# The last norm of the final four token tiles: its reciprocal root moved from GpSimd to ScalarE and VectorE

## The chip, the cores and the metric

The kernel runs on one core of a Trainium2 chip. The metric is the device time of one execution in microseconds (us), as the median of three runs. TensorE (PE in the profile, PEld for its weight loads), VectorE (DVE), ScalarE (ACT) and GpSimd (POOL) work side by side and wait for each other by semaphores; SyncE (SP) issues the transfers, all of them on one queue (q1).

## The reference

The model is one decoder layer over 2048 tokens of width 1024, in float32: a gated linear attention, then a gated feed-forward block with a causal convolution. Each is followed by a residual and a layer norm:

```
def layer_norm(x, g, b):
    mu  = mean(x, -1);  var = mean((x - mu)**2, -1)
    return (x - mu) * rsqrt(var + 1e-5) * g + b

def post_norm_residual(x, cs, w_mod, b_mod, ln_gain, ln_bias, sublayer):
    shift, scale, gate = split(cs @ w_mod + b_mod, 3)
    y = sublayer(x * (1 + scale) + shift)
    return layer_norm(ALPHA * x + (1 + gate) * y, ln_gain, ln_bias)
```

What matters here is the very last step: the layer norm behind the down projection of the feed-forward block. Its result is the output.

## The kernel before

Every large product is made of three matmuls on a float32 operand that is split into a high and a low part (`split`, lines 107 to 111, and `mm3`, lines 113 to 116). The feed-forward block uses a seven-product scheme for 2 x 2 blocks (`ORDER`, `INTO`). The down projection (lines 1321 to 1381) walks over two halves `p` of the tokens and, in each, over the seven products `i`. A product fills four PSUM banks, one for each token tile `t` of 128 rows, and at its end `evict(t)` (line 1345) adds the bank to the accumulator `acc` in SBUF, one column half of 512 at a time.

For a product that completes a token tile (`whole`), the eviction also sums the row into `sm` (`accum_out`), and `ln2` (line 1299) makes the norm from that sum: GpSimd scales it, ScalarE squares and sums, GpSimd takes the power -1/2, VectorE makes the two column halves `y`, SP stores them. These `ln2` calls wait in a list, `work`, and are taken up between the matmuls of the next product.

The last product of the second half (`p == 1`, `i == 2`) is `outer`: here the loop over tiles is the outer one. The 33 matmuls of tile 0 come first, then its eviction and its norm, then tile 1, and so on; so only the norm of tile 3 has no matmuls behind it. Two of the four `ln2` calls that product 3 left in `work` are taken up inside tile 0, the other two inside tile 1. The norm of these last four tiles is `ln2_last` (line 1278). It takes mean and variance from `bn_stats` and `bn_aggr` on VectorE (the statistics of columns 0 to 511 are made ahead, line 1363), then calls `rsqrt_eps` (line 173), two GpSimd instructions: add 1e-5 (line 174), then the power -1/2 (line 175). Beside them VectorE makes (a - mean) * gain for both column halves (line 1290); then, for each half, times the reciprocal root plus the bias (line 1294) and a store (line 1295).

The eviction in `outer` carries the row sum too (line 1347), though `ln2_last` does not read it.

The program orders instructions by a planner: it simulates the engines, takes what is ready by the order of the text, and obeys the added edges of `order(later, earlier)` (line 76). Tiles come from pools. The pools on the left side of SBUF lie one behind the other, `const` first, then `smp`, `rawp`, `hlp`, `t2p`, `zp` and the pools of the stages (`ab`, later `up`); each small tile takes a multiple of 32 bytes per partition. The buffers of `rawp`, `hlp`, `t2p` and `zp` begin at multiples of 256 bytes. The tile `U` of the pool `up` has 1032 floats, 4128 bytes, and two buffers: the second begins 32 bytes past a multiple of 256. In the stage's first loads, the four pairs of `xs` (line 302 to 309) use these two buffers in turn. The pools `actp`, `ur` and `gp` lie on the right side.

Of the kernel before, what the change touches and what calls it, by code (L numbers as in the profile page):

```python
# [8 lines left out]
F32 = mybir.dt.float32  # L9
F32R = mybir.dt.float32r  # L10
U32 = mybir.dt.uint32
AF = mybir.ActivationFunctionType
ALU = mybir.AluOpType
# [3 lines left out]
P = 128  # L17
# [17 lines left out]
EPS = 1e-5  # L35
# [4 lines left out]
def kernel(  # L40
# [22 lines left out]
    nc = tc.nc  # L63
    load = nc.sync.dma_start
    store = nc.sync.dma_start

    const = ctx.enter_context(tc.tile_pool(name="const", bufs=1))
# [8 lines left out]
    def order(later, earlier):  # L76
        tc.add_manual_dep(later.ins, earlier.ins.name,
                          mybir.DependencyInfo(mybir.DependencyClass.NoSync, mybir.DependencyReason.DATA),
                          reason="issue order")
# [4 lines left out]
    def psum(tag, bufs=1):  # L84
        return ps.tile([P, 512], F32, tag=tag, name="ps_" + tag, bufs=bufs)
# [27 lines left out]
    def mm3(po, a, b, first, last, resumed=False):  # L113
        nc.tensor.matmul(po, a[0], b[0], start=first, stop=False, skip_group_check=resumed)  # L114
        nc.tensor.matmul(po, a[0], b[1], start=False, stop=False, skip_group_check=resumed)  # L115
        return nc.tensor.matmul(po, a[1], b[0], start=False, stop=last, skip_group_check=resumed)  # L116
# [52 lines left out]
    nc.vector.memset(still.bitcast(F32), 1.0)  # L169
    mhalf = const.tile([P, 4], F32, name="mhalf")  # L170
    nc.vector.memset(mhalf, -0.5)

    def rsqrt_eps(o, i):
        nc.gpsimd.tensor_scalar(o, i, EPS, None, op0=ALU.add)
        nc.gpsimd.tensor_tensor(o, o, mhalf[:, 0:o.shape[1]], op=ALU.pow)
# [202 lines left out]
    if True:  # L378
# [75 lines left out]
        for n, (dk, more) in enumerate(PE_ROWS):  # L454
            wk = mod_row(start[0][0], dk)
            for c in range(4):
                i = nc.tensor.matmul(pm0[:, c:c + 1], wk[:, c // 2, c % 2 * P:c % 2 * P + P], cs[:, dk:dk + 1],
                                     start=n == 0 and c == 0, stop=False, skip_group_check=True)
# [453 lines left out]
        for tb in range(NTB):  # L912
            last = tb + 1 == NTB
            b = 32 * tb
# [303 lines left out]
    outr = out.rearrange("(t p) d -> t p d", p=P)  # L1218
    ORDER = (0, 1, 4, 5, 6, 3, 2)

    def row(i):
        if i < 2:
            r = gp.tile([P, D], F32, tag="G", name="row0") if i == 0 else ur.tile([P, D], F32, tag="h3", name="row1")
            load(r, lnrow[i:i + 1].partition_broadcast(P))
            nc.vector.tensor_scalar(r, r, ALPHA, None, op0=ALU.mult)
            return r
        hs = []
        for half in range(2):
            hs.append(ur.tile([P, 512], F32, tag="hid", name=f"row{i}", bufs=6))
            load(hs[-1], lnrow[i:i + 1, half * 512:half * 512 + 512].partition_broadcast(P))  # L1230
        return hs
# [28 lines left out]
    def d_get(q):  # L1260
        while len(dloaded) < min(q + 4, len(groups)):
            d_load()
        while len(dready) < min(q + 3, len(groups)):
            d_split()
        return dready[q]
# [12 lines left out]
    def ln2_last(p, b, t):  # L1278
        a, sm = acc.pop((p, b, t))
        st = sts.pop()  # L1280
        nc.vector.bn_stats(st[:, 1], a[:, 512:1024])
        mv = smp.tile([P, 2], F32, tag="mv", name="mv")
        nc.vector.bn_aggr(mv, st)
        rs = smp.tile([P, 2], F32, tag="rs", name="rs")
        rsqrt_eps(rs[:, 0:1], mv[:, 1:2])
        ys = []
        for half in range(2):
            cs_ = slice(half * 512, half * 512 + 512)
            y = t2p.tile([P, 512], F32, tag="t2", name="y")
            nc.vector.scalar_tensor_tensor(y, a[:, cs_], mv[:, 0:1], rows[2][half], op0=ALU.subtract, op1=ALU.mult)  # L1290
            ys.append(y)
        for half in range(2):
            cs_ = slice(half * 512, half * 512 + 512)
            nc.vector.scalar_tensor_tensor(ys[half], ys[half], rs[:, 0:1], rows[3][half], op0=ALU.mult, op1=ALU.add)
            store(outr[p * 8 + b * 4 + t][:, cs_], ys[half])

    sts = []

# [26 lines left out]
    rows = [row(i) for i in range(4)]  # L1325
    work = [(init_acc, 0, b, t) for b in range(2) for t in range(4)]
    for p in range(2):
        bank = {"A": [None] * 4, "C": [None] * 4}
        for i in ORDER:
            kind, b, half, whole = INTO[i]  # L1330
            cs_ = slice(half * 512, half * 512 + 512)
            fresh = i in (0, 1, 4)
            ng = (NP + 1) // 2
            outer = p == 1 and i == ORDER[-1]

            def mms(t, gi, got):
                n = min(2, NP - 2 * gi)
                h, w = got
                for k in range(n):
                    o = k * 512  # L1340
                    mm3(bank[kind][t], (h[:, 0, o + t * P:o + t * P + P], h[:, 1, o + t * P:o + t * P + P]),
                        (w[:, 0, o:o + 512], w[:, 1, o:o + 512]),
                        fresh and gi == 0 and k == 0, gi == ng - 1 and k == n - 1, not fresh)

            def evict(t):
                a, sm = acc[p, b, t]
                acc_out = {"accum_out": sm[:, half:half + 1]} if whole else {}
                nc.vector.scalar_tensor_tensor(a[:, cs_], bank[kind][t], 1.0, a[:, cs_],
                                               op0=ALU.mult, op1=ALU.add, **acc_out)
                if outer:  # L1350
                    ln2_last(p, b, t)
                elif i in (3, 2):
                    work.append((ln2, p, b, t))

            if fresh:
                bank[kind] = [psum("mm" if kind == "A" else "w", 4) for t in range(4)]
            if i == 3 and p == 0:
                work += [(init_acc, 1, 0, t) for t in range(4)]
            if outer:
                got = [d_get(q + gi) for gi in range(ng)]  # L1360
                for t in range(4):
                    sts.append(smp.tile([P, 2, 6], F32, tag="bst", name="bst"))
                    nc.vector.bn_stats(sts[-1][:, 0], acc[p, b, t][0][:, 0:512])
                    for gi in range(ng):
                        mms(t, gi, got[gi])
                        if gi % 3 == 1 and work:
                            f, *a_ = work.pop(0)
                            f(*a_)
                    evict(t)
            else:  # L1370
                for gi in range(ng):
                    got = d_get(q + gi)
                    if work and (gi > 0 or work[0][0] is init_acc):
                        f, *a_ = work.pop(0)
                        f(*a_)
                    for t in range(4):
                        mms(t, gi, got)
                        if gi == ng - 1:
                            evict(t)
            q += ng  # L1380
        work += [(init_acc, 1, 1, t) for t in range(4)] if p == 0 else []
# [58 lines left out]
```

## Time and profile before

| | |
|---|---|
| median of 3 runs | 2142.64 us (2141.45 to 2144.62) |
| the profiled execution | 2140.49 us, of which the span from first to last instruction is 2138.5 us |
| granted TensorE clock | 0.999 |
| busy: PE, DVE, ACT, POOL | 99%, 66%, 42%, 5% of the span |

The profile is that of one execution. A start is counted from the first instruction. Where a timeline row has "x2", it holds two instructions, and its length is that of both. What stands in brackets is the idle time of the engine just before, and who ended it.

### The profile page before, as it was taken

The page shows a single profiled execution, that of the slowest core. Times are in us where ns is not written, and L with a number is a line of the kernel's source. Part 1 is how long each engine was busy: PE and PEld are TensorE (multiplying, and loading weights), DVE is VectorE, ACT ScalarE, POOL GpSimd, SP SyncE. Part 2 cuts the span into 40 slices and gives each one's busy share as a digit, 9 for nine tenths or more (in the row PEclk, how much of TensorE's full clock was granted, in tenths as well). Part 3 has the DMA queues.
Part 4 walks back from the last instruction along what each step waited for, and adds up shares of the span by engine and source line. Part 5 has one row for each costly group of instructions (what it writes and reads, how often), then busy time and mean ns, then how long its engine had stood idle before and what let it go on. Part 6 is the DMA issues. An engine that isn't in the chain of part 4 may idle for free.

```text
span 2138.5 us, 26756 instructions
## 1 busy us (share of the span) xinstructions
PE 2123.3 (99%) x9917; PEld 1770.1 (83%) x9917; DVE 1421.9 (66%) x2013; ACT 892.9 (42%) x1356; POOL 115.9 (5%) x258
## 2 busy tenths in 40 slices
PE   9999999999999999999999999999999999999998
PEld 7888888888888888888888888888888888888886
DVE  7876576434743553878777778666666797578557
ACT  4655453334333343544444454333333433344332
POOL 0010100010001000000000000000000000021003
PEclk9999999999999999999999999999999999999999
DMA  8577886665866766777855469878778897677662
GB/s 314 172 266 259 316 324 228 241 247 176 290 233 243 261 239 234 252 262 282 307 190 183 176 214 341 287 254 279 252 263 277 267 321 276 193 246 253 190 204 89
DMA packets 155106, 529.28 MB, mean 247 GB/s; under 512 B 17664, under 2 KB 21888, under 8 KB 134752
## 3 DMA queue, kind: packets, MB, share of 16 engines
q1 hardware_dynamic: 154976, 527.58, 70.2%
q8 instruction: 78, 1.28, 0.2%
q14 instruction: 52, 0.43, 0.1%
HBM read 364.72 MB, written 162.79 MB: 247 GB/s over the span
## 4 chain that ended last, share of the span: by engine, by line
PE 89%; DVE 4%; DMA 4%; ACT 2%; issue 1%; SPq 0%; POOL 0%; POOLq 0%; DVEq 0%; ACTq 0%
PE ps_mm L114 21%; PE ps_mm L116 21%; PE ps_mm L115 21%; PE ps_w L115 8%; PE ps_w L116 8%; PE ps_w L114 8%; DMA raw<-in_wab_dram 2%; DVE hl L111 1%; DMA mraw<-in_mws_dram 1%; PE ps_w L864 1%; ACT hl L108 1%; PE ps_w L813 1%; PE ps_w L622 0%; DVE macc L234 0%; DMA xraw<-in_xT_dram 0%
## 5 line engine op out<-in xcount | busy, mean ns | idle before, releaser
L114 PE MATMUL ps_mm<-xc,hl 128*128 128x512 f32 x704 | 274.3, 390 | 0.0
L115 PE MATMUL ps_mm<-xc,hl 128*128 128x512 f32 x704 | 273.9, 389 | 0.0
L116 PE MATMUL ps_mm<-xc,hl 128*128 128x512 f32 x704 | 273.9, 389 | 0.0
L114 PE MATMUL ps_mm<-xm,hl 128*128 128x512 f32 x496 | 195.0, 393 | 0.6 <-DVE v L111 0.6
L116 PE MATMUL ps_mm<-xm,hl 128*128 128x512 f32 x496 | 193.6, 390 | 0.0
L115 PE MATMUL ps_mm<-xm,hl 128*128 128x512 f32 x496 | 193.6, 390 | 0.0
L114 PEld LDWEIGHTS ps_mm<-xc,hl 128*128 128x128 f32 x704 | 132.1, 188 | 27.5 <-ACT u L1031 0.2
L116 PEld LDWEIGHTS ps_mm<-xc,hl 128*128 128x128 f32 x704 | 132.1, 188 | 27.4
L115 PEld LDWEIGHTS ps_mm<-xc,hl 128*128 128x128 f32 x704 | 132.1, 188 | 27.3
L1045 DVE SCALAR_TENSOR_TENSOR ct<-U,cw_sb,ct 128x512 f32<-128x512 f32 x176 | 131.7, 748 | 22.1 <-ACT ct L1039 20.6
L114 PE MATMUL ps_w<-xc,hl 128*128 128x512 f32 x352 | 136.9, 389 | 0.0
L115 PE MATMUL ps_w<-xc,hl 128*128 128x512 f32 x352 | 136.9, 389 | 0.0
L116 PE MATMUL ps_w<-xc,hl 128*128 128x512 f32 x352 | 136.9, 389 | 0.0
L108 ACT CAST dhl<-raw 128x1024 fp32r<-128x1024 f32 x57 | 60.0, 1052 | 153.2 <-PE ps_mm L116 96.0
L1031 ACT COPY u<-ps_mm 128x512 f32<-128x512 f32 x88 | 51.4, 584 | 154.9 <-PE ps_mm L116 153.0
L108 ACT CAST hl<-raw 128x1024 fp32r<-128x1024 f32 (+1 forms) x73 | 70.0, 966 | 106.0 <-PE ps_mm L116 42.3
L111 DVE TENSOR_TENSOR dhl<-raw,dhl 128x1024 fp32r<-128x1024 f32 x57 | 69.6, 1221 | 65.3 <-ACT dhl L108 65.3
L111 DVE TENSOR_TENSOR hl<-raw,hl 128x1024 fp32r<-128x1024 f32 (+1 forms) x73 | 81.0, 1118 | 47.9 <-ACT hl L108 47.8
L114 PEld LDWEIGHTS ps_mm<-xm,hl 128*128 128x128 f32 x496 | 93.3, 188 | 19.9 <-DVE v L111 1.0
L116 PEld LDWEIGHTS ps_mm<-xm,hl 128*128 128x128 f32 x496 | 93.2, 188 | 19.9 <-issue 0.2
L115 PEld LDWEIGHTS ps_mm<-xm,hl 128*128 128x128 f32 x496 | 93.3, 188 | 18.1 <-issue 0.2
L114 PE MATMUL ps_mm<-dhl 128*128 128x512 f32 x264 | 102.7, 389 | 0.0
(246 smaller groups left out, 4996.8 us busy)
## 6 DMA issues: line engine op xcount, KB each, us to landing
hl<-wq_d SPq DMA_DIRECT2D x82, 1024.0 KB, 5.0
hc_d<-ct SPq DMA_DIRECT2D x154, 256.0 KB, 2.6
raw<-hc_d SPq DMA_DIRECT2D x70, 512.0 KB, 4.4
draw<-wc_d SPq DMA_DIRECT2D x70, 512.0 KB, 4.8
wq_d<-hl SPq DMA_DIRECT2D x32, 1024.0 KB, 5.2
raw<-in_wab_dram SPq DMA_DIRECT2D x46, 512.0 KB, 5.8
wu<-in_wup_dram SPq DMA_DIRECT2D x44, 512.0 KB, 5.7
wg<-in_wup_dram SPq DMA_DIRECT2D x44, 512.0 KB, 4.1
```

The lines of the kernel that those rows point to most:

```text
L108: accs["copy"] = nc.scalar.copy(h, src)
L111: return nc.vector.tensor_tensor(l, src if lsrc is None else lsrc, h.bitcast(F32), op=ALU.subtract)
L114: nc.tensor.matmul(po, a[0], b[0], start=first, stop=False, skip_group_check=resumed)
L115: nc.tensor.matmul(po, a[0], b[1], start=False, stop=False, skip_group_check=resumed)
L116: return nc.tensor.matmul(po, a[1], b[0], start=False, stop=last, skip_group_check=resumed)
L813: nc.tensor.transpose(pt[:, s * P:s * P + P], on[:, s, e * P:e * P + P], ident)
L864: nc.tensor.transpose(pt[:, t * P:t * P + P], src, ident)
L1031: return t, nc.scalar.copy(t, po)
L1045: nc.vector.scalar_tensor_tensor(ct, U[:, o + i:o + i + 512], cw_sb[:, j, i:i + 1], ct, op0=ALU.mult, op1=ALU.add)
```

## The change

A constant tile `eps` of one column is added behind `mhalf`. In `ln2_last`, ScalarE takes the square root of variance + eps (the constant as its bias operand), VectorE the reciprocal of that; an `order` edge puts the reciprocal behind the first product of column half 0. Each column half is then finished and stored before the next is begun. In `evict`, the row sum is left out where `outer` holds. `rsqrt_eps` stays, for the norms of the attention and of the first residual.

```
     nc.vector.memset(mhalf, -0.5)
+    eps = const.tile([P, 1], F32, name="eps")
+    nc.vector.memset(eps, EPS)
...
         nc.vector.bn_aggr(mv, st)
+
         rs = smp.tile([P, 2], F32, tag="rs", name="rs")
-        rsqrt_eps(rs[:, 0:1], mv[:, 1:2])
+        nc.scalar.activation(rs[:, 1:2], mv[:, 1:2], AF.Sqrt, bias=eps)
         ys = []
         for half in range(2):
             cs_ = slice(half * 512, half * 512 + 512)
             y = t2p.tile([P, 512], F32, tag="t2", name="y")
-            nc.vector.scalar_tensor_tensor(y, a[:, cs_], mv[:, 0:1], rows[2][half], op0=ALU.subtract, op1=ALU.mult)
-            ys.append(y)
-        for half in range(2):
-            cs_ = slice(half * 512, half * 512 + 512)
-            nc.vector.scalar_tensor_tensor(ys[half], ys[half], rs[:, 0:1], rows[3][half], op0=ALU.mult, op1=ALU.add)
-            store(outr[p * 8 + b * 4 + t][:, cs_], ys[half])
+            i = nc.vector.scalar_tensor_tensor(y, a[:, cs_], mv[:, 0:1], rows[2][half], op0=ALU.subtract, op1=ALU.mult)
+            if half == 0:
+                order(nc.vector.reciprocal(rs[:, 0:1], rs[:, 1:2]), i)
+            i = nc.vector.scalar_tensor_tensor(y, y, rs[:, 0:1], rows[3][half], op0=ALU.mult, op1=ALU.add)
+            store(outr[p * 8 + b * 4 + t][:, cs_], y)
...
-                acc_out = {"accum_out": sm[:, half:half + 1]} if whole else {}
+                acc_out = {"accum_out": sm[:, half:half + 1]} if whole and not outer else {}
```

## Rows read from the trace of the kernel before

**Rows 1.** The page: span and busy time of each engine.
```profile
span 2138.5 us, 26756 instructions
PE 2123.3 (99%) x9917; PEld 1770.1 (83%) x9917; DVE 1421.9 (66%) x2013; ACT 892.9 (42%) x1356; POOL 115.9 (5%) x258
```

**Rows 2.** PE's waits: us in total, times, longest; first and last of nine.
```profile
PE ps_mm L657 <- ACT hl L108: 1.7, 1, 1.7
...
PE ps_mm L114 <- DVE z L843: 0.2, 1, 0.2
```

**Rows 3.** The timeline from the last matmuls on: start, us, engine, line, operation.
```profile
2130.26 0.39 PE L116 MATMUL ps_w<-hl 128*128 128x512 f32 x1
2130.68 0.69 DVE L1348 SCALAR_TENSOR_TENSOR acc<-ps_w,acc 128x512 f32<-128x512 f32 x1
2131.30 0.08 DVE L1348 DVE_READ_ACCUMULATOR acc<-ps_w,acc 128x1 f32 x1
2131.41 0.69 DVE L1281 BATCH_NORM_STATS2 bst<-acc 128x6 f32<-128x512 f32 x1
2132.14 0.21 DVE L1283 BATCH_NORM_AGGREGATE mv<-bst 128x2 f32<-128x12 f32 x1
2132.39 1.41 DVE L1290 SCALAR_TENSOR_TENSOR y<-acc,mv,row 128x512 f32<-128x512 f32 x2
2132.44 0.77 POOL L174 TENSOR_SCALAR rs<-mv 128x1 f32<-128x1 f32 x1 [3.30 <-DVE mv L1283]
2133.29 0.93 POOL L175 TENSOR_TENSOR rs<-rs,mhalf 128x1 f32<-128x1 f32 x1
2134.25 1.42 DVE L1294 SCALAR_TENSOR_TENSOR y<-y,rs,row 128x512 f32<-128x512 f32 x2 [0.45 <-POOL rs L175]
2135.03 0.99 SPq L1295 DMA_DIRECT2D out_dram<-y  x2
```

**Rows 4.** VectorE's timeline in tile 2: its last two instructions.
```profile
2129.18 1.41 DVE L1294 SCALAR_TENSOR_TENSOR y<-y,rs,row 128x512 f32<-128x512 f32 x2 [0.45 <-POOL rs L175]
```

**Rows 5.** Source line 1290: duration in ns, least/median/most.
```profile
L1290 DVE SCALAR_TENSOR_TENSOR y<-acc,mv,row x8: 745/749/753, 2112.2 to 2133.1; 128x512 f32<-128x512 f32 x8
```

**Rows 6.** Groups by line and shape: busy us, mean ns, idle us before.
```profile
L495 DVE TENSOR_TENSOR B<-lnc,md 128x8 f32<-128x8 f32 x1 | 0.2, 159 | 0.0
L171 DVE MEMSET mhalf<- 128x4 f32 x1 | 0.1, 62 | 0.0
L163 ACT ACTIVATE cs<-c_sb 128x8 f32<-128x8 f32 x1 | 0.2, 208 | 0.5 <-DMA c_sb<-in_cT_dram 0.5
L1039 ACT ACTIVATE ct<-U,cb_sb,cw_sb 128x512 f32<-128x512 f32 x88 | 71.6, 813 | 49.0 <-DVE U L326 48.4
L1049 ACT ACTIVATE ct<-ct 128x512 f32<-128x512 f32 x88 | 55.7, 633 | 68.8 <-DVE ct L1045 68.8
L724 ACT ACTIVATE sr<-ps_mm 128x512 f32<-128x512 f32 x32 | 19.1, 596 | 36.5 <-PE ps_mm L116 36.4
L724 ACT ACT_TABLE_LOAD x8 | 10.3, 1283 | 0.1
```

**Rows 7.** ScalarE's last instruction (2107 to 2140), and VectorE's aggregate of tile 0.
```profile
2108.56 0.18 ACT L1304 ACTIVATION_READ_ACCUMULATOR sq<-acc,lsm 128x1 f32 x1
2111.97 0.21 DVE L1283 BATCH_NORM_AGGREGATE mv<-bst 128x2 f32<-128x12 f32 x1
```

**Rows 8.** A window: busy us by engine, clock, DMA share, GB/s.
```profile
200.00:300.00 100.00, 98.46 (x469) 81.16 (x467) 70.77 (x110) 47.26 (x66) 6.40 (x18) 1.00 0.86 319
```

**Rows 9.** The chain, 0 to 60: its two transfers (start, us).
```profile
2.16 4.70 DMA mraw<-in_mws_dram
6.88 10.30 DMA mraw<-in_mws_dram
```

**Rows 10.** Loads into `U` buffers: first (847.7 to 848.2), second (864 to 866.6).
```profile
xs<-xm_d SPq DMA_DIRECT2D x1, 512.0 KB, 3.2
xs<-xt_d SPq DMA_DIRECT2D x1, 512.0 KB, 3.6
```

## The prediction

> **What bounds the kernel now.** I read the page first: PE is busy for 2123.3 of 2138.5 us [rows 1]. The view of PE's waits says the same from the other side: it waited nine times, from 1.7 us down to 0.2 [rows 2]. So VectorE, ScalarE and GpSimd count only where PE has nothing left to do, and that is behind the last matmul. The timeline there is one chain [rows 3]. The last matmul ends at 2130.65 (2130.26 + 0.39), the eviction of tile 3 starts at 2130.68, and until the span ends at 2138.5 there are 7.9 us in which nothing runs beside the chain. The chain is: eviction, statistics, aggregate, GpSimd's two instructions (0.77 and 0.93 us), two finishing products on VectorE (1.42 us for both), the last store. VectorE makes its first two products (2132.39, 1.41 for both) beside GpSimd, then waits 0.45 us. The norms of tiles 0 to 2 lie beside the matmuls of the next tile; that of tile 2 ends at 2130.59 (2129.18 + 1.41) [rows 4], 0.09 us before the eviction of tile 3 starts. That cover is thin, so what a norm costs VectorE in the earlier tiles must be watched too.
>
> **The change part by part.**
>
> The sum left out of the eviction. The eviction takes 0.69 us; its accumulator read starts at 2131.30 and takes 0.08, and the statistics start at 2131.41 [rows 3]. The statistics read what the eviction writes, so they must wait for its end in any case. A dependent pair on VectorE is seen just below: statistics end at 2132.10, aggregate starts at 2132.14, 0.04 us later. The eviction ends at 2131.37; plus 0.04 is 2131.41, the start that it has already. The read is hidden in that gap. I take 0; the other end is 0.11 us gained (all the time from the read's start to the statistics).
>
> The root on ScalarE. GpSimd started 0.09 us after the aggregate's end (2132.35 to 2132.44) [rows 3]; I take the same for ScalarE. No Sqrt of one column stands in the trace. The nearest row is the 128x8 ACTIVATE of 0.208 us; a column operand costs about 0.09 (0.813 with two of them against 0.633 with none) [rows 6]. That makes 0.30, and with 0.03 to hand over, the root is there at 2132.77. VectorE comes to the reciprocal only behind the first product, by the order edge: two products take 1.41 and one takes 0.749 [rows 3, 5], so the next instruction starts 0.66 after the first, at 2133.05. The root has 0.28 us to spare, so its cost is 0 on the path. If the cover goes, each microsecond beyond that is paid in full. Queued behind the waiting Sqrt on ScalarE is nothing but the next Sqrt: its last other instruction ends at 2108.74 [rows 7].
>
> The function table. ScalarE loads a table when it changes between groups of functions, 1.283 us each, and it does so ahead of the wait: at line 724 the load has 0.1 us of idle time before it, while the ACTIVATEs of that line waited 36.4 us for PE [rows 6]. Sqrt is used nowhere before, so one load is due. ScalarE is idle from 2108.74 to 2112.18, when tile 0's aggregate ends [rows 7]: 3.4 us, in which the load fits. Later tiles find the table there. On the path: 0. Other end: a load inside the last tile, 2132.44 + 1.28 + 0.30 + 0.03 = 2134.05 for the root, 1.00 us behind 2133.05.
>
> On this point the Trainium skill speaks against the change: "ScalarE: Activation LUTs", section "What ACT_TABLE_LOAD costs", has a switch to another set of functions cost a load and a drain, 2.66 us together, and counts sqrt in a set of its own. The trace agrees on the load (1283 ns) and does not show the drain. By the page's figure the switch would still fit into the 3.4 us; put into the last tile it would make the root 2.4 us late, and the estimate of the end 2.2 us later than before.
>
> The order of the column halves. Reciprocal at 2133.05. It is not in the trace; between the MEMSET of 0.062 and the aggregate of 0.21 the nearest is a small TENSOR_TENSOR of 0.159 [rows 3, 6]. I take 0.16. The product that finishes half 0 needs it: 2133.05 + 0.16 + 0.04 = 2133.25. The first product of half 1 depends on nothing: 0.66 later, 2133.91 to 2134.66. Its finish waits for it: 2134.70 to 2135.45. Before, it ended at 2134.25 + 1.42 = 2135.67 [rows 3]. Gain: 0.22 us. With the reciprocal at 0.06 it is 0.32, at 0.21 it is 0.17. The planner may also put the first product of half 1 ahead of the reciprocal, if it counts the root as late: then 2133.05 to 2133.80, reciprocal 2133.71 to 2133.87, finishes from 2133.91 and 2134.57, end 2135.32, gain 0.35.
>
> The stores. Both are issued by SP, 0.99 us for the two with the wait between them [rows 3]. The last is issued when the last finish ends, before and after; the first goes out 1.0 us earlier (half 0 done at 2134.00 instead of 2135.00), which moves nothing at the end. No DMA is added.
>
> Tiles 0 to 2. Each norm loses VectorE's wait of 0.45 and gains a reciprocal and one dependent gap, the same 0.22 net. That widens the 0.09 us margin and stays off the path. GpSimd loses eight instructions that nobody else waits for.
>
> The constant. One MEMSET of some 0.06 us on VectorE at the start, where it is idle later on, 0. Its column takes 32 bytes ahead of every pool on the left side, so raw, hl, z and most other buffers begin 32 bytes past a multiple of 256, as every second `U` buffer does already. The two `U` buffers bound what that costs a transfer: 3.2 us into the first, 3.6 into the second [rows 10], so between nothing and 12%, with other traffic in both. A transfer that is 12% longer would still be hidden while the 16 DMA engines are busy for 0.86 of a dense stretch [rows 8]: it takes 1 / 0.86, 16%, before they are full. Not hidden is the start, where the chain holds 15.0 us of transfers (4.70 + 10.30) [rows 9]: 12% is 1.8 us. I take 0, by the side of the 88% that would be hidden anyway and because the loads that the chain names (into `actp`) don't move.
>
> On the same point, the Trainium skill, "DMA: Bandwidth & Descriptors", section "How a descriptor splits into AXI transactions", lets a piece that doesn't begin at a multiple of 256 bytes cost one transaction more. For a row of 4096 bytes that is 17 for 16, 6%, so an estimate of 0.9 us at the start; the rows above neither show nor exclude it.
>
> **The sum.** 0 + 0 + 0 - 0.22 + 0 + 0. The profiled execution took 2140.49 us, 2.0 more than its span; after the change it would take 2140.27. The median of the runs shown is 2.15 above the profiled execution, and I carry that over: 2142.64 - 0.22 = 2142.4.
>
> **The rivals.**
> - Half 1 goes ahead of the reciprocal: gain 0.35, 2142.3. For it: the planner's choice is not visible beforehand. Against: the text's order and the root's 0.28 us in hand. Chance 0.17.
> - The tail keeps its length: the root takes 0.22 us longer than its cover (0.28 + 0.22 = 0.50 more than I took), because handing over to ScalarE and back costs more than it did with GpSimd. 2142.6. Against it: 0.09 us from VectorE to GpSimd [rows 3]. Chance 0.12.
> - The table is loaded in the last tile's chain: +1.00 - 0.22 = +0.78, 2143.4, slower. Against it: the load at line 724 runs before the wait, and three Sqrts come first. Chance 0.06.
> - The 32 bytes lengthen the transfers, slower than before: at the bound of 12% the start grows by 1.8 us, 2144.2. From 29% on (4.3 / 15.0) it would pass 0.2%, and from 16% on it would show as waits of PE between 200 and 300 us too. Chance 0.06, of which 0.03 above 0.2%.
> - The new instructions shift the planner's order far from the end, and PE's waits change by 5 us either way. PE's nine waits hold little that could be won [rows 2]: 0.01 faster; slower 0.01.
>
> My forecast has the remaining 0.57.
>
> **How the numbers follow.** What a measurement of this kernel can tell from no change is 0.2%, 4.3 us. All cases but the last and half of the one before lie within 2 us of the time before, that is, within 0.2%: 0.57 + 0.17 + 0.12 + 0.06 + 0.03 = 0.95. The runs of before spread over 3.2 us, and the profiled one lies 1 us below them, so a median of three can be off by itself; I move 0.02 of it outwards: faster 0.03, same 0.93, slower 0.04. The range takes the forecast, the rivals up to 2144.2 and the spread of the runs: 2140.0 to 2144.6.
>
> **What would show it.** In the changed profile: the statistics of tile 3 start 0.73 us after the eviction, with no accumulator read; a Sqrt of about 0.3 us beside the first product; one table load, before 2112; reciprocal 0.66 after the first product; the last finish 3.06 us after the first product starts, instead of 3.28. It would be wrong if the reciprocal idles for ScalarE, if VectorE is not done with tile 2 when the last matmul ends, or if PE's waits in the first 300 us grow.

## The result, and the profile after

| | median | runs | profiled execution / span |
|---|---|---|---|
| before | 2142.86 us | 2141.45 to 2144.62, 4 | 2140.49 / 2138.5 us |
| after | 2166.08 us | 2165.09 to 2167.15, 4 | 2167.15 / 2165.4 us |

The ratio after/before is 1.0111, 95% interval 1.0099 to 1.0123: the kernel became 23 us slower. The prediction of 2142.4 us was wrong, the measured time lies far above its range (up to 2144.6), and the case that had a chance of 0.93, no change, did not come. The two spans differ by 26.9 us. Two executions that took two and over five times as long as the rest, one of e4 (4239 us) and one of the kernel before on the chip of e5 to e8 (11932 us), are left out of every number below.

The page of the kernel after, span and busy time of each engine, answers to [rows 1]:

```profile
span 2165.4 us, 26752 instructions
PE 2153.0 (99%) x9917; PEld 1771.5 (82%) x9917; DVE 1423.9 (66%) x2014; ACT 895.7 (41%) x1361; POOL 109.6 (5%) x250
```

TensorE has as many matmuls as before, 9917, and is busy 29.7 us longer with them. The other engines' sums hardly moved. TensorE's waits after (total, times, longest; seven of them, first and last) leave nothing to explain it, as against [rows 2]:

```profile
PE ps_mm L434 <- DVE mhalf L171: 1.4, 1, 1.4
...
PE ps_mm L114 <- DVE v L111: 0.2, 1, 0.2
```

So the time went neither to waiting nor to more work. Where it went, the windows show (us, PE busy with its number of matmuls, PEld, DVE, ACT, POOL, granted clock, DMA share, GB/s). First the kernel before:

```profile
400.00:880.00 480.00, 479.54 (x2385) 403.45 (x2384) 231.40 (x382) 177.21 (x341) 29.39 (x68) 1.00 0.68 244
900.00:1700.00 800.00, 800.00 (x3548) 662.76 (x3547) 589.75 (x783) 331.29 (x448) 18.64 (x70) 1.00 0.73 255
1720.00:2080.00 360.00, 360.00 (x1590) 298.10 (x1589) 249.71 (x291) 149.32 (x166) 20.27 (x32) 1.00 0.72 240
```

and after, with the dense stretch of [rows 8] ahead:

```profile
200.00:300.00 100.00, 99.22 (x450) 79.75 (x449) 70.66 (x110) 46.24 (x65) 6.41 (x18) 1.00 0.86 319
400.00:880.00 480.00, 479.13 (x2357) 395.40 (x2357) 223.41 (x372) 172.98 (x338) 29.30 (x66) 1.00 0.66 237
900.00:1700.00 800.00, 800.00 (x3497) 653.55 (x3496) 585.22 (x780) 323.59 (x438) 21.88 (x75) 1.00 0.72 251
1720.00:2080.00 360.00, 360.00 (x1588) 297.82 (x1587) 258.16 (x302) 150.99 (x170) 20.93 (x32) 1.00 0.74 248
```

Read the count of matmuls in brackets. From 900 to 1700 us (the up projection) TensorE is busy in every microsecond of both kernels, at a granted clock of 1.00 in both, and got through 3548 matmuls before and 3497 after: 51 fewer, 1.4%. From 1720 to 2080 us, in the down projection, it is 1590 and 1588: no difference. A stretch from one run of 72 matmuls shows it too. TensorE's timeline after (start, length):

```profile
464.74 0.40 PE L114 MATMUL ps_mm<-hl,xm 128*128 128x512 f32 x1
464.98 0.39 PE L115 MATMUL ps_mm<-hl,xm 128*128 128x512 f32 x1
465.21 0.40 PE L116 MATMUL ps_mm<-hl,xm 128*128 128x512 f32 x1
465.44 0.39 PE L114 MATMUL ps_mm<-hl,xm 128*128 128x512 f32 x1
...
```

and the same in the kernel before:

```profile
458.16 0.39 PE L115 MATMUL ps_mm<-hl,xm 128*128 128x512 f32 x1
458.38 0.39 PE L116 MATMUL ps_mm<-hl,xm 128*128 128x512 f32 x1
458.61 0.39 PE L114 MATMUL ps_mm<-hl,xm 128*128 128x512 f32 x1
458.84 0.39 PE L115 MATMUL ps_mm<-hl,xm 128*128 128x512 f32 x1
...
```

A matmul's own length (0.39 to 0.40 us) says little, since they overlap; the distance from one start to the next is its price. I call this distance a step. Three of them take 0.70 us after (464.74 to 465.44) and 0.68 before (458.16 to 458.84); the mean over the 72 is 233.3 ns after and 226.8 before.

The end itself went almost as predicted. The timeline after from the last matmul on, against [rows 3]:

```profile
2156.61 1.41 DVE L1296 SCALAR_TENSOR_TENSOR y<-y,rs,row 128x512 f32<-128x512 f32 x2
...
2157.61 0.39 PE L116 MATMUL ps_w<-hl 128*128 128x512 f32 x1
2158.03 0.69 DVE L1350 SCALAR_TENSOR_TENSOR acc<-ps_w,acc 128x512 f32<-128x512 f32 x1
2158.76 0.69 DVE L1283 BATCH_NORM_STATS2 bst<-acc 128x6 f32<-128x512 f32 x1
2159.49 0.21 DVE L1285 BATCH_NORM_AGGREGATE mv<-bst 128x2 f32<-128x12 f32 x1
2159.73 0.29 ACT L1288 ACTIVATE rs<-mv,eps 128x1 f32<-128x1 f32 x1 [4.22 <-DVE mv L1285]
2159.73 0.75 DVE L1293 SCALAR_TENSOR_TENSOR y<-acc,mv,row 128x512 f32<-128x512 f32 x1
2160.40 0.16 DVE L1295 RECIPROCAL rs<-rs 128x1 f32<-128x1 f32 x1
2160.47 0.73 DVE L1293 SCALAR_TENSOR_TENSOR y<-acc,mv,row 128x512 f32<-128x512 f32 x1
2161.12 1.41 DVE L1296 SCALAR_TENSOR_TENSOR y<-y,rs,row 128x512 f32<-128x512 f32 x2
```

From the start of the eviction to the end of the last product it took 4.99 us before (2130.68 to 2135.67) and takes 4.50 now (2158.03 to 2162.53): 0.49 us won, in a kernel that lost 27 elsewhere.

### The profile page after: what moved, and what is told of

It is laid out like the page before. It is cut to its first block, busy times and chain, and to the rows that moved or that the text cites. A ratio compares the mean times of both kernels' runs of the same rounds, so it can differ in the third digit from the quotient of the medians.

```text
span 2165.4 us, 26752 instructions
## 1 busy us (share of the span) xinstructions
PE 2153.0 (99%) x9917; PEld 1771.5 (82%) x9917; DVE 1423.9 (66%) x2014; ACT 895.7 (41%) x1361; POOL 109.6 (5%) x250
## 4 chain that ended last, share of the span: by engine, by line
PE 91%; DVE 3%; DMA 3%; ACT 1%; issue 1%; POOL 0%; SPq 0%; DVEq 0%; ACTq 0%
PE ps_mm L114 22%; PE ps_mm L116 22%; PE ps_mm L115 22%; PE ps_w L115 7%; PE ps_w L116 7%; PE ps_w L114 7%; DMA raw<-in_wab_dram 1%; DMA mraw<-in_mws_dram 1%; PE ps_w L866 1%; PE ps_w L815 1%; DVE hl L111 0%; PE ps_w L624 0%; ACT hl L108 0%; DMA xp<-xm_d 0%; PE ps_w L545 0%
## 5 line engine op out<-in xcount | busy, mean ns | idle before, releaser
L114 PE MATMUL ps_mm<-xm,hl 128*128 128x512 f32 x496 | 197.5, 398 | 0.2 <-DVE v L111 0.2
L116 PE MATMUL ps_mm<-xm,hl 128*128 128x512 f32 x496 | 196.5, 396 | 0.0
L115 PE MATMUL ps_mm<-xm,hl 128*128 128x512 f32 x496 | 196.1, 395 | 0.0
L116 PEld LDWEIGHTS ps_mm<-xc,hl 128*128 128x128 f32 x704 | 132.2, 188 | 29.7
L115 PE MATMUL ps_w<-xc,hl 128*128 128x512 f32 x352 | 138.6, 394 | 0.0
L114 PE MATMUL ps_w<-xc,hl 128*128 128x512 f32 x352 | 138.6, 394 | 0.0
L116 PE MATMUL ps_w<-xc,hl 128*128 128x512 f32 x352 | 138.4, 393 | 0.0
```

## The experiments

Three theories stood at first; the expectations below go by their numbers. In the first two, the `eps` column is to blame, since it moves the buffers of the left side by 32 bytes. Theory 1, relative place: TensorE is slower wherever the moving operand (the one that streams through) lies on one side and the weights on the other, so that they no longer begin alike. Theory 2, absolute place: whatever begins 32 bytes past a multiple of 256 is slower by itself. Theory 3, the rival: the changed norms and evictions shift the planner's order far from the end. "+23" and the like below is the median less that of the kernel before on the same chip.

**e1: the column alone.** The kernel before, with the constant allocated and filled, and used by nothing.

```
     nc.vector.memset(mhalf, -0.5)
+    eps = const.tile([P, 1], F32, name="eps")
+    nc.vector.memset(eps, EPS)
```

> The kernel before with the eps column allocated and filled, and nothing else of the change: its value is not used. It moves the left-side buffers by 32 bytes. Theory 1, relative place: TensorE reads the moving operand of one matmul and the weights of the next at the same time, and a step costs 227 ns when both begin at the same remainder of bytes and 231 to 235 when one is 32 bytes off; so matmuls with one operand on the left and one on the right are slow: the whole loss stays, 2166 to 2167 us. Theory 2, absolute place: whatever begins 32 bytes past a multiple of 256 is slower to read or to transfer: 2166 to 2167 too. Theory 3, the new tail or the planner's order makes the loss: 2142.9.

Measured: 2165.24 us (2164.16 to 2166.61), ratio 1.0111 [1.0095, 1.0128]. Its window from 900 to 1700:

```profile
900.00:1700.00 800.00, 800.00 (x3497) 653.55 (x3496) 583.56 (x778) 322.87 (x438) 21.85 (x75) 1.00 0.72 251
```

The same 3497 matmuls as after. A column that nobody reads costs all of it.

**e2: the change without the column.** The whole change, with `eps` as a fifth column of `mhalf`, whose slot of 32 bytes has room for it; no buffer moves.

```
-    mhalf = const.tile([P, 4], F32, name="mhalf")
-    nc.vector.memset(mhalf, -0.5)
-    eps = const.tile([P, 1], F32, name="eps")
+    mhalf = const.tile([P, 5], F32, name="mhalf")
+    nc.vector.memset(mhalf[:, 0:4], -0.5)
+    eps = mhalf[:, 4:5]
...
```

> The whole change, but eps takes a fifth column of mhalf, whose 32 bytes it already has: no buffer moves. Theories 1 and 2: the loss is gone, 2142.4, and the tail from the last eviction to the last finish is 4.50 us instead of 4.99. Theory 3: 2166.

Measured: 2140.72 us (10 runs), ratio 0.9996 [0.9987, 1.0006], against 2141.61. The window from 900 to 1700:

```profile
900.00:1700.00 800.00, 800.00 (x3548) 662.76 (x3547) 589.30 (x782) 331.72 (x448) 18.74 (x70) 1.00 0.73 255
```

and VectorE's timeline in the norm of tile 3 (start, length, the idle time ahead in brackets):

```profile
2130.46 0.69 DVE L1350 SCALAR_TENSOR_TENSOR acc<-ps_w,acc 128x512 f32<-128x512 f32 x1 [0.60 <-PE ps_w L116]
2131.19 0.69 DVE L1283 BATCH_NORM_STATS2 bst<-acc 128x6 f32<-128x512 f32 x1
...
2133.55 1.41 DVE L1296 SCALAR_TENSOR_TENSOR y<-y,rs,row 128x512 f32<-128x512 f32 x2
```

All 3548 matmuls are back with the new norm in place, so the norm and the planner's order have no part in the loss. The built programs say the same: the matmuls of before, after, e1 and e2 stand in one and the same order, by the names and sizes of their operands. The tail takes 4.50 us as after (2130.46 to 2134.96). This is the version to keep: what the change was predicted to do, and no measurable difference in time, since 0.49 us is 0.02%.

**e3, e8: which side moves.** The right side ends in a pad of 56 floats. With 48, the buffers on the right (`actp`, `ur`, `gp`) begin 32 bytes higher. In e3 this is added to the whole change, so both sides moved by 32; in e8 it is the only edit to the kernel before.

```
-    pad.tile([P, 56], F32, name="pad")
+    pad.tile([P, 48], F32, name="pad")
```

> The whole change, and the pad tile on the right side 32 bytes smaller, so that the right-side buffers too begin 32 bytes past a multiple of 256. Theory 1: both operands have the same remainder again, steps of 227 ns, 2142.4 us. Theory 2: still more buffers are off, so 2166 or more, 2180 if the right side costs as much as the left. Theory 3: 2166.

> The kernel before with the right-side buffers moved up by 32 bytes and the left side where it was, 32 bytes the other way round than in the changed kernel. Theory 1: the same matmuls are slow: 2155 to 2166 us. If only the left side's place counts: 2142.

Measured: e3 2143.16 us (10 runs), 1.0007 [0.9998, 1.0017]; e8 2167.66 us, 1.0118 [1.0102, 1.0134]. The window of e3:

```profile
900.00:1700.00 800.00, 800.00 (x3547) 663.00 (x3546) 589.09 (x783) 331.06 (x447) 21.11 (x74) 1.00 0.73 255
```

and of e8:

```profile
900.00:1700.00 800.00, 800.00 (x3492) 652.27 (x3491) 583.24 (x777) 322.87 (x437) 21.88 (x75) 1.00 0.72 251
```

Either side alone costs 24 to 26 us, both together nothing that can be told. So it is not where a buffer begins that counts, but how the two sides lie to each other. It also excludes transfers as the cause: in e3 the buffers of both sides are moved by 32 bytes for their transfers too, and the time is back.

**e4, e5, e9, e10: by how much.** The whole change with one more constant, so that the left side moves by 64, 128, 96 and 160 bytes: 8, 24, 16 and 32 floats. e4's edit:

```
+    more = const.tile([P, 8], F32, name="more")
+    nc.vector.memset(more, 0.0)
```

> The whole change and one more unused constant of 32 bytes, so that the left-side buffers move by 64 bytes against the kernel before. Theory 1 with a period of 64 bytes: 2142.4 us; with a longer period (128 or 256): 2166, steps of 231 to 235 ns. Theory 2, with multiples of 256: 2166; theory 3: 2166.

> The whole change and one more unused constant of 96 bytes: the left-side buffers move by 128 bytes against the kernel before. Theory 1a, relative place with a period of 128 bytes: 2142 us. Theory 1b, a period of 256: slow, 2155 to 2166 us, with steps of 231 to 235 ns wherever one operand is on the left and one on the right. That 64 bytes cost less (2159) than 32 (2165) leaves both open.

> The whole change and one more unused constant of 64 bytes: the left-side buffers stand 96 bytes (of 256) off the right-side ones. Relative place with a period of 256: slow, 2155 to 2168 us, fewer matmuls than the 3548 of the kernel before from 900 to 1700 us. If only multiples of 32 that are not multiples of 64 cost the full price, it is near the 2165 of 32 bytes and not near the 2159 to 2161 of 64 and 128.

> The same with 128 bytes more: 160 bytes off, which is also 96 bytes short of 256. Relative place with a period of 256: slow, 2155 to 2168 us; if the sign of the difference does not matter, as 96. If the price falls towards 256, nearer 2155.

| left side moved by | us | more than before | ratio |
|---|---|---|---|
| 32 (after) | 2166.08 | +23.2 | 1.0111 [1.0099, 1.0123] |
| 64 (e4, three runs) | 2158.82 | +17.2 | 1.0079 [1.0062, 1.0096] |
| 96 (e9) | 2168.07 | +26.0 | one run |
| 128 (e5) | 2160.77 | +18.9 | 1.0085 [1.0069, 1.0101] |
| 160 (e10) | 2171.48 | +29.4 | one run |

Every distance that was tried, up to 160 bytes, costs 17 to 29 us. 64 and 128 are the cheaper ones, and none is free.

**e6: 256 bytes apart.** The kernel before; `cs` is made in place of `c_sb` and `ba_sb` and `ng_sb` share a slot, which moves the left side down by 64 bytes; the pad of 8 floats moves the right side up by 192. Both now begin at remainder 192 of 256, and stand 256 bytes further apart.

```
-    cs = const.tile([P, KT], F32, name="cs")
+    cs = c_sb
...
-    ba_sb = const.tile([P, NH], F32, name="ba_sb")
-    ng_sb = const.tile([P, 2], F32, name="ng_sb")
+    ba_ng = const.tile([P, NH + 2], F32, name="ba_ng")
+    ba_sb, ng_sb = ba_ng[:, 0:NH], ba_ng[:, NH:NH + 2]
...
-    pad.tile([P, 56], F32, name="pad")
+    pad.tile([P, 8], F32, name="pad")
```

> The kernel before with its two sides 256 bytes further apart: two pairs of small constants share a slot (left side 64 bytes down), the pad tile is 192 bytes smaller (right side 192 up). Both sides then begin 192 bytes past a multiple of 256. Theory 1 with a period of 256 bytes or a divisor of it: as before, 2142. With a period of 512 the kernel before would itself be half a period off, and this one on it: another time than 2142, either way by 10 us or more. Theory 2, absolute place: 2166 or more.

Measured: 2143.09 us (10 runs), 1.0006 [0.9996, 1.0016], and in the window:

```profile
900.00:1700.00 800.00, 800.00 (x3547) 662.77 (x3546) 588.66 (x782) 330.92 (x448) 19.46 (x72) 1.00 0.74 255
```

The 3547 of e3 again. 256 bytes are as good as none, and 64 and 128 are not, so the price goes by the remainder of 256.

**e7: one pool.** The kernel before, with a tile of 32 bytes ahead in the pool `up`: of the left side only the up projection's buffers move.

```
+                up.tile([P, 8], F32, name="shim")
```

> The kernel before with 32 unused bytes ahead of the buffers of the pool up alone, so that two buffers of the same side stand 32 bytes apart: hl (weights) and xc (moving) in products 0, 1, 4 and 5 of the feed-forward block. Theory 1: those 2112 matmuls take 231 to 235 ns instead of 227, 10 to 16 us in all, 2152 to 2158; the stages before 900 us and the down projection keep their pace, as do products 2, 3 and 6. If what counts is one side of SBUF against the other, nothing changes: 2142.

Measured: 2164.68 us, 1.0102 [1.0084, 1.012]: more than expected. Its windows:

```profile
400.00:880.00 480.00, 479.29 (x2389) 403.26 (x2388) 231.63 (x383) 178.95 (x346) 29.48 (x68) 1.00 0.67 245
900.00:1700.00 800.00, 800.00 (x3468) 647.62 (x3467) 576.53 (x764) 319.13 (x433) 17.70 (x69) 1.00 0.72 249
1720.00:2080.00 360.00, 360.00 (x1582) 296.66 (x1581) 254.66 (x297) 146.72 (x166) 20.27 (x32) 1.00 0.73 245
```

The stages ahead of the up projection keep their pace (2389 to 2385 of before), and the up projection loses 80 matmuls, where after lost 51. Here `xc` of `up` at 32 meets `hl` at 0 in 2112 steps of 233.7 ns instead of 226.8 (worked out as in the table below): 14.6 us. The rest slowed too, though their own operands agree: `xc` on the right side with `hl`, 0 and 0, to 229.7, and the down projection by 8 matmuls in 360 us. Such steps stand beside others whose operands differ, or whose remainders are others; more on that under the table. All matmuls of the two stages together took 21.4 us longer than before, of the 23.8 by which the span grew.

**Steps by place.** The trace has each matmul's start, the built program each operand's byte address. I matched the two lists by line and shape (9867 pairs) and took the mean step in ns, by the remainders mod 256 of moving operand / weights:

| moving, weights (matmuls after) | before | after | e3 | e8 |
|---|---|---|---|---|
| `xm`, `hl` (1485) | 0/0: 230.1 | 0/32: 235.7 | 32/32: 232.2 | 32/0: 235.1 |
| `xc` on the right side, `hl` (1056) | 0/0: 226.8 | 0/32: 233.6 | 32/32: 226.8 | 32/0: 233.6 |
| `hl`, `gated` (757) | 0/0: 230.3 | 32/0: 235.4 | 32/32: 229.8 | 0/32: 234.4 |
| `hl`, `xm` (721) | 0/0: 230.2 | 32/0: 234.3 | 32/32: 229.7 | 0/32: 234.7 |
| `xc` of `up`, `hl` (2068) | 0/0: 226.8 | 32/32: 228.3 | 32/32: 226.8 | 0/0: 228.9 |
| `dhl`, `dhl` (1368, down projection) | 0/0: 226.7 | 32/32: 226.7 | 32/32: 226.7 | 0/0: 226.7 |

Where the remainders differ, 97 to 100% of the steps exceed 229 ns; in the last row 1% do. The rows at 230 in the kernel before are no slower kind: 84 to 90% of their steps are at most 229 ns too, and waits and the first steps behind a change of operands raise the mean. So in these rows read the increase and not the level. The increases over before, times the counts: 1485 x 5.6 + 1056 x 6.8 + 757 x 5.1 + 721 x 4.1 + 2068 x 1.5 ns = 8.3 + 7.2 + 3.9 + 3.0 + 3.1 = 25.5 us. Another 484 of the up projection with 2.2 more, and 88 at its changes of operand with 8 more, make 1.8 us: 27.3 in all, for 26.9 us of span plus the 0.5 that the tail won. The loss is accounted for. In the fifth row the operands agree, and 27% of the steps are slow nevertheless. They are the first ones of a group: the first five behind a group whose operands differ (230, 236, 228, 233, 231, then 226), and the first seven behind the products of `xc` and `h3`, both on the right side at 0 (230, 224, 231, 236, 228, 232, 231, then 227). There the operands of both groups agree, only at another remainder.

**e11: the sum kept.** e2 with the sum at the eviction.

```
-                acc_out = {"accum_out": sm[:, half:half + 1]} if whole and not outer else {}
+                acc_out = {"accum_out": sm[:, half:half + 1]} if whole else {}
```

> The whole change with eps in the spare column of mhalf (no buffer moves), but with the row sum kept at the last evictions. By the prediction's step the sum costs nothing at the end: statistics start 0.73 us after the eviction with and without it, 2141 us. The other bound was 0.11 us.

Measured: 2142.39 us in one run, against 2142.11 of before. VectorE's timeline:

```profile
2133.31 0.68 DVE L1350 SCALAR_TENSOR_TENSOR acc<-ps_w,acc 128x512 f32<-128x512 f32 x1
2133.92 0.08 DVE L1350 DVE_READ_ACCUMULATOR acc<-ps_w,acc 128x1 f32 x1
2134.04 0.69 DVE L1283 BATCH_NORM_STATS2 bst<-acc 128x6 f32<-128x512 f32 x1
```

From eviction to statistics 0.73 us with the read, and 0.73 without it in e2 (2130.46 to 2131.19): the read lies in the gap that the dependent pair has anyway. The whole run of one execution is not a measure of 0.1 us, so only this distance is read.

## Why the prediction was wrong, point by point

- **The sum at the eviction: 0.** Right, 0.73 us with and without it.
- **The root on ScalarE: 0.30 long, 0.28 to spare.** Right: 0.29 us. It started 0.03 us after the aggregate's end (2159.70), not 0.09, and ended at 2160.02, 0.38 before the reciprocal's start at 2160.40.
- **The table: one load, off the path.** Right. ScalarE's timeline after, before tile 0's norm:

```profile
2135.91 0.19 ACT L1306 ACTIVATION_READ_ACCUMULATOR sq<-acc,lsm 128x1 f32 x1
2136.12 1.28 ACT L1288 ACT_TABLE_LOAD   x1
2139.56 0.29 ACT L1288 ACTIVATE rs<-mv,eps 128x1 f32<-128x1 f32 x1 [2.16 <-DVE mv L1285]
```

  The load follows the last instruction of the old functions at once, and 2.16 us of idle time follow it. Of the drain that the Trainium skill counts beside the load ("ScalarE: Activation LUTs", "What ACT_TABLE_LOAD costs"), the row shows nothing: 0.02 us lie ahead of the load, though the idle time behind it could hide one. Earlier in the same trace a load stands between two functions with no wait that could hide a drain. There the next function starts 0.01 us after the load's end:

```profile
327.09 0.63 ACT L522 ACTIVATE az<-mn 128x512 f32<-128x512 f32 x1
327.74 1.28 ACT L511 ACT_TABLE_LOAD   x1
329.03 0.63 ACT L526 ACTIVATE az<-az 128x512 f32<-128x512 f32 x1
```

- **The order of the halves: 0.22 won.** The sign was right, the size 0.49, and the order was neither my forecast nor the rival: the planner put the first product of half 1 behind the reciprocal, but ahead of both finishes. By my own durations, that is a start at 2133.05 + 0.16 = 2133.21 for it, the two finishes 0.66 and 1.32 later, and an end at 2133.21 + 1.32 + 0.75 = 2135.28: 0.39 won. Of the other 0.10, 0.09 is the reciprocal: the row is 0.16 long, as I took it, but the next product, which doesn't need it, starts 0.07 us after it. The last finish ended 2.80 us after the first product's start (2159.73 to 2162.53), where I had 3.06.
- **Tiles 0 to 2: off the path, with a wider margin.** Right in some executions only. In the kernel after, tile 2's norm ended at 2158.02 (2156.61 + 1.41) and the last matmul at 2158.00: the margin of 0.09 us was gone, and nothing was lost by it. A wait came up that I had not listed and that the kernel before does not have. VectorE's timeline in tile 1:

```profile
2144.93 0.75 DVE L1311 SCALAR_TENSOR_TENSOR y<-acc,lsm,row 128x512 f32<-128x512 f32 x1
2147.12 0.75 DVE L1311 SCALAR_TENSOR_TENSOR y<-acc,lsm,row 128x512 f32<-128x512 f32 x1 [1.45 <-DMA out_dram<-y]
```

  A product of an `ln2` asks for a `y` buffer whose store has not landed yet. This wait uses up the margin: in e2 it took 0.86 us, and 0.60 us of margin were left; in the kernel after 1.45 us, and nothing was left. In e3, with the same new norm, it took 1.79 us. There the last matmul ends at 2136.12, and the eviction starts 0.30 us later, behind tile 2's finishes, instead of 0.03:

```profile
2135.09 1.41 DVE L1296 SCALAR_TENSOR_TENSOR y<-y,rs,row 128x512 f32<-128x512 f32 x2
...
2135.73 0.39 PE L116 MATMUL ps_w<-hl 128*128 128x512 f32 x1
2136.42 0.68 DVE L1350 SCALAR_TENSOR_TENSOR acc<-ps_w,acc 128x512 f32<-128x512 f32 x1
```

  So more than half of the 0.49 us won can be lost again at this place.
- **The constant: "I take 0". This is the step that failed.** I had seen that its column moves nearly all buffers of the left side by 32 bytes, and asked only what that does to transfers. On them I was right: the share of the DMA engines from 200 to 300 us is 0.86 at 319 GB/s as in [rows 8], and the loss stays away in e3, where they all go to moved buffers. The two transfers at the head of the chain go to the right side, so it is e3 that tests them. Its chain (start, length):

```profile
2.17 4.60 DMA mraw<-in_mws_dram
6.79 10.75 DMA mraw<-in_mws_dram
```

  15.35 us together, against 15.0 in [rows 9]. The estimate of 0.9 us by the Trainium skill's rule on pieces that begin off a multiple of 256 bytes ("DMA: Bandwidth & Descriptors", "How a descriptor splits into AXI transactions") is more than these rows show, 0.35. That tells nothing from none: where these transfers go to unmoved buffers they took 15.1 us in the kernel after and 14.6 in e2. But TensorE reads its operands from the same buffers, and of that the prediction says nothing. The term was 23 us by the medians, 27 by the spans.
- **The rivals.** That the 32 bytes cost time had the right place, and the wrong mechanism and size: transfers, 1.8 us. The planner's rival is excluded by e1, which is slow with the tail unchanged, and by e2, which is not slow with the tail changed.
- **The signs to look for.** None of the three that I named points at the loss. The reciprocal did not wait for ScalarE, and PE's waits in the first 300 us did not grow (6.2 us in all before, 3.2 after). By the letter one sign came, as VectorE was done with tile 2 0.02 us after the last matmul; but the eviction started 0.03 us after the matmul, as before. All three look at waits. For a kernel whose bound engine is busy 99% of the time, the list lacked the one term that counts, the pace of that engine. The 29.7 us that it was busy longer are 1.4% of the 2123.3 in [rows 1], and over a hundred times the 0.22 that I worked out.

**What stays open.** That the relative place mod 256 sets the step is what e1 to e10 show, for the distances tried. How is not. Two reads go on at once, since TensorE loads the next weights while it streams (PEld is busy 82% of the span beside PE), and with 32 bytes a matmul whose own operands agree is slow, 235 ns, when the next one's weights differ (44 of 44 in e1). But with 64 bytes the same 44 take 226 ns, so this is not the whole of it; nor do I know why the matmuls behind such a group need five to seven steps to recover, nor why 64 and 128 bytes are cheaper than 32, 96 and 160. The distances 96 and 160 rest on one run each, and 192 was not tried.

## What to carry to other kernels

Before adding even one small constant, see which buffers it moves, and keep the moving operands and the weights at the same remainder mod 256 bytes within the partition: use a free column of an existing slot, or pad the other side by as much. Where one engine is busy 99% of the time, compare its pace (work done in the same window, steps of the same kind) ahead of all waits. A change at the very end of a program can cost its time far from there.

## What the hardware showed that I had not expected

- A 128x512 float32 matmul takes a step of 226.8 ns where moving operand and weights begin at the same remainder mod 256 bytes, and 233.6 where they differ by 32 (`xc` on the right side with `hl`), at the same granted clock of 1.00. On the whole kernel 32 to 160 bytes cost 0.8 to 1.4%, and 256 nothing that can be told.
- A 128x1 reciprocal of 0.16 us holds VectorE up for 0.07 us only, when the next instruction doesn't need it.
- An accumulator read of 0.08 us costs nothing where the next instruction depends on the eviction (0.73 us from start to start either way).
